# A hybrid decoder layer: its front ordered by a list scheduler, conv sums in PSUM, q over both partition halves

## The chip, the core and the metric

The kernel runs on one core of a Trainium2 chip. The metric is device microseconds of one execution, as the median of several runs. TensorE does the matrix products, VectorE and ScalarE work on SBUF and PSUM, GpSimd works on SBUF alone, and SyncE (SP) issues the loads. Each engine takes its instructions in the order in which the kernel was written, so the place of an instruction in its engine's queue matters as much as its length.

## What is computed

One decoder layer on 512 tokens of width 1024, all in float32. The mixer has an attention group of 8 heads of 64 (with 512 tokens and blocks of 256 it comes to causal softmax attention) and a conv group of 512 channels with 31 taps. Both are joined by one output projection. An MLP with a squared ReLU follows, then a last norm.

```python
xn = rms_norm(h, g_mix_norm)
q, k, v, u = split(xn @ w_in, [512, 1024, 1536])        # u: 1024 columns, a and gate
attn = moba_attention(partial_rope(q), partial_rope(k), v)
a, gte = split(u + b_glu, 2)
c = causal_depthwise_conv(a * sigmoid(gte), w_dw) + b_dw   # 31 taps, 512 channels
conv = swish(layer_norm(c))
h = h + concat([attn, conv]) @ w_out
ff = square(relu(rms_norm(h, g_mlp_norm) @ w_mlp_in))
return rms_norm(h + ff @ w_mlp_out, g_final)
```

## The kernel before

Every large product keeps float32 precision by splitting both operands into a high and a low part and doing three matmuls (`mm3`, lines 158 to 160). A weight unit is 128 x 1024: SP loads it into one of four `raw` buffers, ScalarE copies the high part `wh` (line 115) and VectorE subtracts to get the low part `wl` (line 116, `split_unit`); there are three buffers of parts.

The front, up to the output projection, runs in this order. x is transposed and split into `xh` and `xl`. Units 0 to 7 give the u columns (`u`), from which `glu` makes four gated conv inputs `hin` of 128 channels x 512 tokens each. Units 8 to 11 give q, 12 to 15 k, 16 to 19 v, each in four PSUM banks, one for 128 tokens. q and k are scaled into SBUF by ScalarE (line 396), rotated by VectorE (lines 402 to 405), transposed on TensorE (line 411) and split again (lines 416, 419). A pair of heads shares 128 partitions: the low part `ql` of a head lies on its own 64, and the high part of q is copied to the other half as well by two transfers that GpSimd issues (line 422). Attention then works on 32 groups (head, 128 tokens): scores (lines 467 to 469: q high with the high and low halves of k, q low on 64 partitions with k high, and the mask), row maximum (476), exponential (483), normalisation on GpSimd (491), transpose (497), split of the probabilities (512, 518), and per head the product with v (530, 531). Half of the output projection (k = 0 to 3, the attention rows) is laid between these; the other half follows with the conv rows.

The conv: blocks 0 and 2 belong to GpSimd. For each tap ScalarE makes a product `ct` (line 313) and GpSimd adds it to the sum in SBUF (line 323). Blocks 1 and 3 belong to VectorE, one instruction a tap: `hin` times the tap plus the sum, all in SBUF (line 300; the first tap is line 294). Both are background work, put between other instructions by `background`, which hands each engine a share of the time of every `mm3` by constants from the table `T`. The attention part is an event list: each step has a place in slots (constants of `T`, such as `rm`, `ex`, `pt`), and the sorted list is the order of issue on all engines. All eight PSUM banks are one rotating pool.

After the front the MLP runs in four chunks (`ff`, `z`), TensorE without a gap, weights split two units ahead.

Of the kernel before, what the change touches and what calls it, by code (L numbers as in the profile page):

```python
# [31 lines left out]
POOL_BLOCKS = (0, 2)  # L32
CHUNK = 8
LAG = 3
# [16 lines left out]
T = {"sh_u": 0.608, "sh_p": 0.984, "c_p": 1.34, "sh_q": 0.576, "sh_k": 0.408, "sh_v": 0.308, "rm": 0.077, "ex": 1.057, "no": 1.206, "pt": 3.026, "ph": 3.551, "pl": 3.667, "vm0": 0.073, "vms": 0.365, "sp18": -2.63, "sp19": 4.368, "tk18": 1.875, "tk19": 4.562, "td0": 0.346, "tds": 0.755, "tp0": 0.806, "tps": 1.188, "mt": 10.032, "vs0": 8.08, "vss": 0.464, "sp20": 5.876, "sp21": 17.846, "sp22": 22.437, "sp23": 35.926, "lst": 0.496, "lsc": 2.037, "lbs": 0.564, "ms": 0.818, "msp": 1.662, "lt0": 15.178, "lb0": 24.678, "sw0": 44.304, "y030": 39.415, "y130": 39.247, "lt1": 19.058, "lb1": 23.299, "sw1": 42.879, "y031": 43.841, "y131": 43.064, "lt2": 20.23, "lb2": 23.114, "sw2": 32.77, "y032": 47.586, "y132": 45.976, "lt3": 20.62, "lb3": 26.779, "sw3": 35.787, "y033": 41.198, "y133": 43.882, "va0": 10.623, "va1": 12.961, "va2": 16.592, "va3": 19.269, "va4": 25.479, "va5": 27.641, "va6": 33.134, "va7": 35.475, "y000": 21.654, "y100": 34.028, "y001": 18.594, "y101": 35.235, "y002": 21.974, "y102": 35.427, "y003": 28.582, "y103": 38.359, "y010": 22.511, "y110": 35.552, "y011": 22.65, "y111": 35.891, "y012": 26.772, "y112": 36.197, "y013": 30.362, "y113": 42.111, "y020": 32.483, "y120": 36.489, "y021": 31.142, "y121": 37.522, "y022": 31.744, "y122": 38.63, "y023": 33.118, "y123": 38.744, "el18": 1, "el19": 0, "el20": 1, "el21": 1, "el22": 1, "el23": 0, "epl0": 0, "epl1": 0, "ems": 1, "esh": 0, "esw": 1, "er0": 0, "er1": 0, "er2": 0, "er3": 0, "rx": 31.357, "px": 0}  # L51
# [3 lines left out]
def hybrid_layer(ctx: ExitStack, tc: tile.TileContext, x, pack, w_in, w_out, g_mlp, w1, w2, g_fin, out):  # L55
# [6 lines left out]
    def acc(name):  # L62
        return psum.tile([P, 512], F32, tag="ps", name=name)

    def bank(name):
        return psum.tile([P, 512], F32, tag="ps", name=name)
# [27 lines left out]
    RAW, SPL = 4, 3  # L94

    def load_unit(pieces=1, between=None):
        n = len(raws)
        if n < len(srcs):
            raw = perm.tile([P, 1024], F32, tag="raw", name=f"raw{n}", bufs=RAW)
# [6 lines left out]
            raws[n] = raw  # L106

    def split_unit(pieces=1, low=nc.vector, between=None):
        n = len(parts)
        if n < len(srcs):  # L110
            hi = perm.tile([P, 1024], FR, tag="wh", name=f"wh{n}", bufs=SPL)
            lo = perm.tile([P, 1024], FR, tag="wl", name=f"wl{n}", bufs=SPL)
# [6 lines left out]
            a = srcs[n].shape[1]  # L119
            parts[n] = (hi.rearrange("p (a b) -> p a b", a=a), lo.rearrange("p (a b) -> p a b", a=a))  # L120
            load_unit()

    def resident_unit(hi, lo):
        n = len(parts)
        raw = raws[n].rearrange("p (a b) -> p a b", a=srcs[n].shape[1])
        nc.scalar.copy(hi, raw)
        eng(f"er{n % 4}").tensor_tensor(lo, raw, f32(hi), op=OP.subtract)
        parts[n] = None
        nunit[0] += 1
        load_unit()  # L130
# [10 lines left out]

    bgq = {"dve": deque(), "pool": deque()}
    credit = {"dve": 0.0, "pool": 0.0}
    share = {"dve": T["sh_u"], "pool": T["sh_p"]}

    def background(us):
        for e, q in bgq.items():
            credit[e] += us * share[e]
            while q and credit[e] >= q[0][0]:
                cost, fn = q.popleft()  # L150
                credit[e] -= cost
                fn()
            if not q:
                credit[e] = min(credit[e], 0.0)

    def mm3(ps, sh, sl, mh, ml, first, last):
# [4 lines left out]
        background(3 * mh.shape[-1] / 2400)  # L161
# [5 lines left out]

    xt = x_tiles("x")
    pk = perm.tile([P, C_END], F32, name="pk")
# [57 lines left out]
    pa = phA.enter_context(tc.tile_pool(name="pa", bufs=1))  # L227


    xh = perm.tile([P, KD, S], FR, tag="xh", name="xh")  # L230
# [24 lines left out]
    def norm1(t):  # L255
        junk = pa.tile([P, D], F32, tag="ptah", name=f"junk{t}", bufs=2)
# [6 lines left out]
    def scales_on_rows():  # L263

        rb = acc("rb")
# [21 lines left out]
    hins, accs = {}, {}  # L287
# [5 lines left out]
    def conv_first(e, acc, i, j, bias):  # L293
        e.tensor_scalar(acc, hins[i][:, j:j + S], wtap(i, j), bias, op0=OP.mult, op1=OP.add)

    def conv_dve(i, j):
        if j == 0:
            conv_first(nc.vector, accs[i], i, 0, pk[:, C_BDW + i:C_BDW + i + 1])
# [5 lines left out]
    AHEAD = 2  # L304
    pool_taps, products = [], []

    def product(n):
        if n < len(pool_taps):
            acc, i, j, first = pool_taps[n]
            tmp = None  # L310
            if not first:
                tmp = pa.tile([P, S], F32, tag="ctmp", name=f"ct{i}_{j}", bufs=AHEAD + 2)
                nc.scalar.activation(tmp, hins[i][:, j:j + S], AF.Copy, scale=wtap(i, j))  # L313
            products.append(tmp)

    def conv_pool(n):
        while len(products) < min(n + 1 + AHEAD, len(pool_taps)):
            product(len(products))
        acc, i, j, first = pool_taps[n]
        if first:  # L320
            conv_first(nc.gpsimd, acc, i, j, pk[:, C_BDW + i:C_BDW + i + 1] if j == 0 else 0.0)
        else:
            nc.gpsimd.tensor_tensor(acc, acc, products[n], op=OP.add)  # L323

    def add_taps(e, i, js, acc):
        for n, j in enumerate(js):
            if e == "pool":
                pool_taps.append((acc, i, j, n == 0))
                bgq[e].append((T["c_p"], lambda n=len(pool_taps) - 1: conv_pool(n)))
            else:  # L330
                bgq[e].append((0.67, lambda i=i, j=j: conv_dve(i, j)))

    def glu(i, zg, za):
        sg = pa.tile([P, S], F32, tag="sg", name=f"sg{i}", bufs=1)
        nc.vector.tensor_mul(sg, zg, rbc)
        nc.scalar.activation(sg, sg, AF.Sigmoid, bias=pk[:, C_BG + 4 + i:C_BG + 5 + i])
        hin = hins[i]
        nc.vector.tensor_mul(hin[:, TAPS - 1:], za, rbc)
        nc.vector.scalar_tensor_tensor(hin[:, TAPS - 1:], hin[:, TAPS - 1:], pk[:, C_BG + i:C_BG + i + 1], sg,
                                       op0=OP.add, op1=OP.mult)  # L340
        accs[i] = pa.tile([P, S], F32, tag="acc", name=f"acc{i}", bufs=4)
        if i in POOL_BLOCKS:
            add_taps("pool", i, range(TAPS), accs[i])
            return
        nd = TAPS - (int(T["px"]) if i == 3 else 0)
        add_taps("dve", i, range(nd), None)
        if nd < TAPS:
            more = pa.tile([P, S], F32, tag="ol", name=f"more{i}", bufs=2)
            add_taps("pool", i, range(nd, TAPS), more)
            join.append(lambda: nc.vector.tensor_add(accs[i], accs[i], more))  # L350

    join = []
    for i in range(4):
        hins[i] = pa.tile([P, TAPS - 1 + S], F32, tag="hin", name=f"hin{i}", bufs=4)
# [5 lines left out]
    tx = [acc(f"tx1{b}") for b in range(4)]  # L360
# [5 lines left out]
    block(z[0], w[0], xh, xl, H1)  # L366
    split_unit()
    block(z[1], w[1], xh, xl, H1)
    glu(0, z[0], z[1])
    split_unit()  # L370
    block(z[2], w[2], xh, xl, H1)
    for n in range(3, 8):
        zn = bank(f"u{n}")
        block(zn, unit(), xh, xl)
        z.append(zn)
# [224 lines left out]
    def take(n):  # L600
        U[n] = unit(0)

# [297 lines left out]
```

## Time and profile before

| | |
|---|---|
| median of 3 runs | 624.48 us (624.02 to 624.49) |
| profiled execution | 623.05 us, its span 621.3 us |
| TensorE busy | 578.2 us (93%), 2768 matmuls |
| VectorE busy | 369.7 us (59%) |
| ScalarE busy | 266.1 us (43%) |
| GpSimd busy | 162.9 us (26%) |

The page's chain of work that ended last is 76% TensorE and 15% VectorE, and its largest line is not a matmul: it is line 300, VectorE's conv taps, with 10% of the span. The shares of busy time are means over stages that differ; the rows below cut the span into such stages. A busy TensorE is not one at its peak: successive starts of matmuls show the pace.

### The profile page before, as it was taken

How to read it: one execution, taken by the hardware profiler on the slowest of the kernel's cores; microseconds unless marked ns; L12 is line 12 of the kernel's file. 1: busy time of each engine (PE TensorE's matmuls, PEld its weight loads, DVE VectorE, ACT ScalarE, POOL GpSimd, SP SyncE). 2: the span in 40 equal slices, each digit the busy share in tenths (PEclk: the TensorE clock that was granted, in tenths of full speed). 3: DMA queues.
4: the chain of work that ended last, by engine and by line, in shares of the span. 5: the costliest groups of instructions: out<-in, count | busy, mean ns of one | idle time of the engine just before them, and what ended most of it. 6: DMA issues, size and time to landing. Idle time of an engine off the chain costs nothing.

```text
span 621.3 us, 7312 instructions
## 1 busy us (share of the span) xinstructions
PE 578.2 (93%) x2768; PEld 476.7 (77%) x2768; DVE 369.7 (59%) x486; ACT 266.1 (43%) x445; POOL 162.9 (26%) x170
## 2 busy tenths in 40 slices
PE   8998692876999999999999999999999999999995
PEld 7986562765767788898888888888888888888884
DVE  4589999999989766746424454431455343345243
ACT  6864263663768773435321144322234222334233
POOL 2496598492887551100000000000000000000002
PEclk9999987896999999999999999999999999999998
DMA  8632122161111156205233322233232333222203
GB/s 265 153 98 66 38 68 67 35 135 34 56 47 35 35 205 169 69 1 170 101 102 101 93 78 102 102 102 101 72 99 101 103 101 102 86 86 99 69 0 137
DMA packets 59380, 57.22 MB, mean 92 GB/s; under 512 B 1872, under 2 KB 42960, under 8 KB 59344
## 3 DMA queue, kind: packets, MB, share of 16 engines
q1 hardware_dynamic: 58512, 54.64, 28.6%
q0 software_dynamic: 544, 1.05, 1.0%
q10 hardware_dynamic: 288, 1.05, 0.4%
q8 instruction: 22, 0.36, 0.2%
q14 instruction: 14, 0.11, 0.1%
HBM read 53.59 MB, written 2.10 MB: 90 GB/s over the span
## 4 chain that ended last, share of the span: by engine, by line
PE 76%; DVE 15%; issue 3%; ACT 2%; POOL 2%; DMA 1%; SPq 0%; POOLq 0%; ACTq 0%; DVEq 0%
DVE acc L300 10%; PE ff L159 9%; PE ff L158 9%; PE ff L160 9%; PE z L159 9%; PE z L158 9%; PE z L160 9%; DVE wl L116 3%; PE y L158 2%; PE y L160 2%; PE y L159 2%; PE u L160 1%; PE u L159 1%; PE u L158 1%; PE pt L497 1%
## 5 line engine op out<-in xcount | busy, mean ns | idle before, releaser
L116 DVE TENSOR_TENSOR wl<-raw,wh 128x1024 fp32r<-128x1024 f32 (+1 forms) x86 | 113.2, 1318 | 100.6 <-ACT wh L115 100.3
L115 ACT CAST wh<-raw 128x1024 fp32r<-128x1024 f32 (+1 forms) x94 | 92.6, 991 | 117.8 <-PE z L160 75.3
L323 POOL TENSOR_TENSOR acc<-acc,ct 128x512 f32<-128x512 f32 x60 | 98.2, 1636 | 23.2 <-ACT ct L313 19.5
L158 PE MATMUL ff<-hTh,wh 128*128 128x512 f32 (+1 forms) x280 | 103.9, 371 | 0.0
L159 PE MATMUL ff<-hTl,wh 128*128 128x512 f32 (+1 forms) x280 | 103.8, 371 | 0.0
L160 PE MATMUL ff<-hTh,wl 128*128 128x512 f32 (+1 forms) x280 | 103.8, 371 | 0.0
L159 PE MATMUL z<-wl,ffh 128*128 128x512 f32 (+1 forms) x264 | 101.0, 383 | 0.0
L158 PE MATMUL z<-wh,ffh 128*128 128x512 f32 (+1 forms) x264 | 101.0, 383 | 0.0
L160 PE MATMUL z<-wh,ffl 128*128 128x512 f32 (+1 forms) x264 | 101.0, 383 | 0.0
L699 POOL TENSOR_SCALAR ms0f<-ms_f 128x1 f32<-128x1 f32 x4 | 0.8, 192 | 328.7 <-ACT f L223 328.7
L300 DVE SCALAR_TENSOR_TENSOR acc<-hin,pk,acc 128x512 f32<-128x512 f32 x60 | 83.0, 1384 | 1.4
L763 DVE TENSOR_TENSOR sq<-rl 128x512 f32<-128x512 f32 x32 | 22.2, 692 | 64.3 <-ACT rl L761 64.3
L158 PEld LDWEIGHTS ff<-hTh,wh 128*128 128x128 f32 x280 | 52.8, 188 | 9.1
L160 PEld LDWEIGHTS ff<-hTh,wl 128*128 128x128 f32 x280 | 52.7, 188 | 9.0
L159 PEld LDWEIGHTS ff<-hTl,wh 128*128 128x128 f32 x280 | 52.8, 188 | 9.0
L158 PEld LDWEIGHTS z<-wh,ffh 128*128 128x128 f32 x264 | 49.6, 188 | 9.8
L160 PEld LDWEIGHTS z<-wh,ffl 128*128 128x128 f32 x264 | 49.6, 188 | 9.7
L159 PEld LDWEIGHTS z<-wl,ffh 128*128 128x128 f32 x264 | 49.6, 188 | 9.6
L761 ACT ACTIVATE rl<-ff 128x512 f32<-128x512 f32 x32 | 19.2, 599 | 82.6 <-PE ff L160 82.6
L313 ACT ACTIVATE ct<-hin,pk 128x512 f32<-128x512 f32 x60 | 41.5, 719 | 17.9 <-POOL acc L323 17.5
L765 DVE TENSOR_TENSOR ffl<-sq,ffh 128x512 fp32r<-128x512 f32 x32 | 22.2, 693 | 21.9 <-ACT ffh L764 21.9
L764 ACT CAST ffh<-sq 128x512 fp32r<-128x512 f32 x32 | 19.8, 620 | 25.5 <-DVE sq L763 25.5
(162 smaller groups left out, 899.5 us busy)
## 6 DMA issues: line engine op xcount, KB each, us to landing
raw<-w SPq DMA_DIRECT2D x64, 512.0 KB, 3.9
raw<-w_in SPq DMA_DIRECT2D x18, 512.0 KB, 3.7
raw<-w_out SPq DMA_DIRECT2D x8, 512.0 KB, 3.7
xr<-x SPq DMA_DIRECT2D x4, 512.0 KB, 5.0
out<-ot SPq DMA_DIRECT2D x8, 256.0 KB, 2.0
x<-x SPq DMA_DIRECT2D x4, 256.0 KB, 4.4
raw<-w_in SPq DMA_DIRECT2D x4, 256.0 KB, 5.9
x<-x SPq DMA_DIRECT2D x2, 512.0 KB, 6.9
```

The source lines that it names most:

```text
L115: nc.scalar.copy(hi[:, c], raws[n][:, c])
L116: low.tensor_tensor(lo[:, c], raws[n][:, c], f32(hi[:, c]), op=OP.subtract)
L158: nc.tensor.matmul(ps, sh, mh, start=first, stop=False)
L159: nc.tensor.matmul(ps, sh, ml, start=False, stop=False)
L160: nc.tensor.matmul(ps, sl, mh, start=False, stop=last)
L300: nc.vector.scalar_tensor_tensor(accs[i], hins[i][:, j:j + S], wtap(i, j), accs[i], op0=OP.mult, op1=OP.add)
L313: nc.scalar.activation(tmp, hins[i][:, j:j + S], AF.Copy, scale=wtap(i, j))
L323: nc.gpsimd.tensor_tensor(acc, acc, products[n], op=OP.add)
L761: nc.scalar.activation(rl, ps, AF.Relu)
L763: nc.vector.tensor_mul(sq, rl, rl)
L764: nc.scalar.copy(ff["h"][:, b], sq)
L765: nc.vector.tensor_sub(ff["l"][:, b], sq, f32(ff["h"][:, b]))
```

## The change

Four things are done to the front; the MLP stays as it is.

- The order. A class `Plan` holds every step of the front from the second half of u to the output projection's first half, with the engine (or two engines to choose from), an estimated duration, the steps it needs and the buffers it uses. `run` is a list scheduler that works at build time: of the steps that can start earliest it takes the one with the longest remaining path. The kernel then issues the steps in that order. `background`, the event list and the table `T` go. Splits of weights may go to VectorE or GpSimd.
- The conv sums of VectorE's blocks 1 and 3 lie in a PSUM bank while they grow; the last tap writes to SBUF. GpSimd's blocks 0 and 2 stay in SBUF.
- q is copied twice side by side for each head before its transpose, so that the high and the low part (`ql`, now 8 heads x 512 tokens on 128 partitions) fill both halves of the partitions. Each 128 tokens of q take 8 transposes instead of 4, and GpSimd's two transfers go. A score takes two full 128-row matmuls and the mask.
- PSUM banks and the buffers of weights get names of their own, so that the scheduler can give them out. Some tiles move in SBUF (the tiles called `shift`), and the scratch for transfers issued by GpSimd is set to 4096.

```diff
+class Plan:
+    def step(self, engines, cost, fn, needs=(), uses=(), bias=0.0, keep=0, shared=False, hot=False):
...
+    def run(self):
+        for s in reversed(self.steps):
+            s["tail"] = min(s["eng"].values()) + max([n["tail"] for n in s["next"]], default=0.0) + 0.1
...
+            e0 = min(best, key=lambda x: x[2])[1]
+            a0 = min(x[2] for x in best if x[1] == e0)
+            s, e, a, c = max((x for x in best if x[1] == e0 and x[2] <= a0 + 0.02), key=lambda x: x[0]["tail"] + x[0]["bias"])
...
-    psum = ctx.enter_context(tc.tile_pool(name="psum", bufs=8, space=bass.MemoryType.PSUM))
+    psum = ctx.enter_context(tc.tile_pool(name="psum", bufs=1, space=bass.MemoryType.PSUM))
...
-        background(3 * mh.shape[-1] / 2400)
...
+        l = plan.step({"dve": 1.23, "pool": 2.2}, 0, lambda: low(nc.gpsimd if l["eng_used"] == "pool" else nc.vector),
+                      needs=[h], uses=[rb, wb], shared=True)
...
-            nc.vector.scalar_tensor_tensor(accs[i], hins[i][:, j:j + S], wtap(i, j), accs[i],
-                                           op0=OP.mult, op1=OP.add)
...
+        cs = ps_buffer(f"cs{i}")
...
+            s = plan.step("dve", 0.8, lambda src=src, j=j, last=last: nc.vector.scalar_tensor_tensor(
+                get(acc) if last else get(cs), src, wtap(i, j), get(cs), op0=OP.mult, op1=OP.add),
+                needs=[s], uses=[cs, acc] if last else [cs])
...
-    ql = pa.tile([P, 4, S], FR, name="ql")
+    ql = pa.tile([P, NH, S], FR, name="ql")
...
+            src = get(b).rearrange("p (h d) -> p h d", h=NH).unsqueeze(2).to_broadcast([P, NH, dup, HD])
+            nc.scalar.activation(tile_of(), src, AF.Copy, scale=rq[t] if nm == "q" else rs[t])
...
-                nc.gpsimd.dma_start(qs[own[1 - a], a::2], qs[own[a], a::2])
...
-        nc.tensor.matmul(sp[:, 0:n], ql[rows, h // 2, tok], ks[rows, h, 0:n], start=False, stop=False)
+                nc.tensor.matmul(p[:, 0:n], ql[:, h, tok], ks[:, h, 0:n], start=False, stop=False)
...
+            s = pe_step(2 * mm(n) + BF16_MASK, scores, uses=[sp], chain=False, keep=KEEP,
+                        needs=[qready[qt, a]] + [kready[t, h % 2] for t in range(qt + 1)] + score_steps[-1:])
...
+                fin.append(pe_step(3 * mm(512), omm, needs=[l, mixready[k]], uses=[y[hf][t], wb], chain=False, keep=KEEP_Y))
...
+    plan.step("sp", 7.0, reload_x, needs=score_steps)
+    order = plan.run()
+    for s in order:
+        s["fn"]()
```

`keep` (2 for scores, 3 for the output projection) is the number of PSUM banks that must stay free before such a step may take one while a head's product with v is outstanding.

## Rows read from the trace of the kernel before

**Rows 1.** The page's busy table: us, share of the span, instructions, by engine.

```profile
PE 578.2 (93%) x2768; PEld 476.7 (77%) x2768; DVE 369.7 (59%) x486; ACT 266.1 (43%) x445; POOL 162.9 (26%) x170
```

**Rows 2.** Stretches: us, busy us (instructions) by engine, TensorE's granted clock, DMA share.

```profile
21.00:57.00 36.00, 35.75 (x192) 30.71 (x190) 29.53 (x25) 18.23 (x27) 24.89 (x15) 1.00 0.28 79
57.00:178.00 121.00, 89.77 (x360) 68.75 (x361) 117.35 (x140) 67.35 (x111) 85.95 (x55) 0.86 0.23 64
178.00:239.00 61.00, 59.99 (x332) 46.44 (x331) 47.52 (x106) 45.71 (x105) 35.54 (x47) 1.00 0.25 87
239.00:613.00 374.00, 374.00 (x1757) 313.84 (x1756) 163.55 (x190) 117.89 (x168) 6.96 (x22) 1.00 0.30 92
```

**Rows 3.** Waits, 57 to 178 us: who waited for whom, us, times, longest.

```profile
PE tpq L411 <- DVE qf L405: 10.0, 1, 10.0
...
PE tpk L411 <- DVE kf L405: 9.2, 1, 9.2
```

**Rows 4.** Groups by line, 57 to 178 us: busy us, mean ns, idle before.

```profile
L300 DVE SCALAR_TENSOR_TENSOR acc<-hin,pk,acc 128x512 f32<-128x512 f32 x52 | 70.5, 1356 | 1.1
L116 DVE TENSOR_TENSOR wl<-raw,wh 128x1024 fp32r<-128x1024 f32 x11 | 20.6, 1876 | 0.4 <-ACT wh L115 0.4
...
L469 PE MATMUL s<-maskb,identb 128*128 128x128 bf16 x9 | 2.1, 230 | 0.0
```

**Rows 5.** Single lines, 21 to 239 us: ns min/median/max, first and last start.

```profile
L300 DVE SCALAR_TENSOR_TENSOR acc<-hin,pk,acc x60: 734/1651/2089, 40.9 to 176.3; 128x512 f32<-128x512 f32 x60
...
L116 DVE TENSOR_TENSOR wl<-raw,wh x17: 1199/2160/2316, 24.8 to 226.3; 128x1024 fp32r<-128x1024 f32 x17
...
L338 DVE TENSOR_TENSOR hin<-u,rbc x4: 681/687/692, 26.7 to 74.5; 128x512 f32<-128x512 f32 x4
...
L610 DVE SCALAR_TENSOR_TENSOR vhl<-v,r,vhl x4: 725/730/739, 177.1 to 179.9; 128x512 fp32r<-128x512 f32 x4
```

**Rows 6.** Timeline of GpSimd and VectorE near 100 us: start, us, what.

```profile
94.07 12.73 POOL L323 TENSOR_TENSOR acc<-acc,ct 128x512 f32<-128x512 f32 x7
...
96.65 6.83 DVE L300 SCALAR_TENSOR_TENSOR acc<-hin,pk,acc 128x512 f32<-128x512 f32 x4
...
107.12 3.12 DVE L300 SCALAR_TENSOR_TENSOR acc<-hin,pk,acc 128x512 f32<-128x512 f32 x4
```

**Rows 7.** Timeline of TensorE and its weight loads around one score group.

```profile
187.01 0.60 PE L497 MATMUL pt<-ident,pr 128*128 128x128 f32 x4
...
187.37 0.47 PE L467 MATMUL s<-ks,qs 128*128 128x512 f32 x1
...
187.77 0.18 PEld L468 LDWEIGHTS s<-ks,ql 64*128 64x128 f32 x1 [0.24 <-issue]
187.77 0.50 PE L468 MATMUL s<-ks,ql 64*128 64x512 f32 x1
...
188.20 0.23 PE L469 MATMUL s<-maskb,identb 128*128 128x128 bf16 x1
```

**Rows 8.** Timeline of TensorE in q's projection, after a wait.

```profile
79.07 0.63 PE L159 MATMUL q<-wl,xh 128*128 128x512 f32 x1
79.50 0.63 PE L160 MATMUL q<-wh,xl 128*128 128x512 f32 x1
```

**Rows 9.** Timeline of TensorE in a product with v.

```profile
181.43 0.39 PE L531 MATMUL o<-pl,vhl 128*128 128x512 f32 x1
181.66 0.34 PE L530 MATMUL o<-ph,vhl 128*128 128x384 f32 x1
```

**Rows 10.** Groups by line and shape, whole span: busy us, mean ns, idle before.

```profile
L571 DVE TENSOR_SCALAR y<-cp,mv,r_ln 128x512 f32<-128x512 f32 x4 | 3.1, 798 | 0.0
...
L396 ACT ACTIVATE qf<-q,rq 128x512 f32<-128x512 f32 x4 | 2.4, 681 | 0.0
...
L422 POOL DMA_DIRECT2D qs<-qs x2 | 1.5, 737 | 1.6 <-ACT qs L416 1.6
```

**Rows 11.** Score matmuls of the high part: ns min/median/max, first and last start.

```profile
L467 PE MATMUL s<-ks,qs x32: 220/350/473, 153.2 to 217.7; 128*128 128x128 f32 x8, 128*128 128x256 f32 x8, 128*128 128x384 f32 x8, 128*128 128x512 f32 x8
```

More of the change, by code (lines that the diff above doesn't have):

```diff
@@ L304, in hybrid_layer @@
[L304 to L323, printed above, removed]
@@ L359, in hybrid_layer @@
     block(z[1], w[1], xh, xl, H0)
-    tx = [acc(f"tx1{b}") for b in range(4)]
+    tx = [bank(f"tx1{b}") for b in range(4)]
     transpose_half(1, tx)
@@ new lines, in hybrid_layer, with u_block, part @@
+    zs, zdone = {}, {}
+    def u_block(n, cols):
+        if n not in zs:
+            zs[n] = held("ps", f"b{n}", z[n]) if n < 3 else ps_buffer(f"u{n}")
+        wb, l = U[n]
+        width = cols.stop - cols.start
+        def part(k0):
+            hi, lo = parts[n]
+            for k in (k0, k0 + 1):
+                mm3(get(zs[n])[:, cols], hi[:, k], lo[:, k], xh[:, k, cols], xl[:, k, cols], k == 0, k == KD - 1)
+        for k0 in range(0, KD, 2):
+            zdone[n] = pe_step(6 * mm(width), lambda k0=k0: part(k0), needs=[l], uses=[zs[n], wb])
@@ L408, in rope_transpose, with project, one @@
-    def rope_transpose(nm, t, qf):
-        tp = bank(f"tp{nm}{t}")
-        for p in range(4):
-            nc.tensor.transpose(tp[:, p * P:(p + 1) * P], qf[:, p * P:(p + 1) * P], ident)
-        tv = tp.rearrange("p (a b) -> p a b", a=4)
+    new_pr = pa_buffers("pr", PR, [P, S])
+    rt = pa.tile([P, 2, NH, 2, HALF], F32, name="rope")
+    rope_last = [None]
+    def project(nm, u0):
+        bk = [ps_buffer(f"{nm}{t}") for t in range(NT)]
+        done = {}
+        def one(t, k):
+            hi, lo = parts[u0 + k // 2]
+            ts = slice(t * P, (t + 1) * P)
+            mm3(get(bk[t]), xh[:, k, ts], xl[:, k, ts], hi[:, k % 2], lo[:, k % 2], k == 0, k == KD - 1)
+        order = [(t, k) for k in range(4) for t in range(NT)] + [(t, k) for t in range(NT) for k in range(4, KD)]
+        for t, k in order:
+            wb, l = U[u0 + k // 2]
+            done[t] = pe_step(3 * mm(512), lambda t=t, k=k: one(t, k), needs=[l], uses=[bk[t], wb])
+        return bk, done
@@ L456, in eng @@
-    def eng(k):
-        return nc.gpsimd if T[k] > 0.5 else nc.vector
-    slots = [(h, qt) for h in range(NH) for qt in range(NT)]
-    scored, probs, pT, tps = {}, {}, {}, {}
-    def scores(h, qt):
-        rows = own[h % 2]
-        n = (qt + 1) * P
-        tok = slice(qt * P, (qt + 1) * P)
-        sp = bank(f"s{h}{qt}")
-        nc.tensor.matmul(sp[:, 0:n], qs[:, h, tok], ks[:, h, 0:n], start=True, stop=False)
-        nc.tensor.matmul(sp[:, 0:n], ql[rows, h // 2, tok], ks[rows, h, 0:n], start=False, stop=False)
-        nc.tensor.matmul(sp[:, tok], identb, maskb, start=False, stop=True)
-        nm = stat(f"nm{h}{qt}")
-        scored[h, qt] = sp, nm
@@ L493, in prob_transpose, with flip @@
-    def prob_transpose(h, qt):
-        pr, _ = probs.pop((h, qt))
-        tp = bank(f"pt{h}{qt}")
-        for j in range(qt + 1):
-            nc.tensor.transpose(tp[:, j * P:(j + 1) * P], pr[:, j * P:(j + 1) * P], ident)
-        tps[h, qt] = tp
+            tp = ps_buffer(f"tpq{t}{a}")
+            def flip(a=a, tp=tp):
+                for h in range(4):
+                    c = (4 * a + h) * P
+                    nc.tensor.transpose(get(tp)[:, h * P:(h + 1) * P], get(qb)[t % 2][:, c:c + P], ident)
@@ L520, in hybrid_layer @@
-    mix, outs = {}, {}
-    def values(h):
-        ph, pl = pT.pop(h)
-        op = bank(f"o{h}")
-        outs[h] = op
-        for j in range(NT):
-            seen = slice(PSTEP * j + j * P, PSTEP * j + S)
-            v = vhl[:, j, h].rearrange("p a d -> p (a d)")
-            nc.tensor.matmul(op[:, j * P:], v, ph[:, seen], start=j == 0, stop=False)
-            nc.tensor.matmul(op[:, j * P:], v, pl[:, seen], start=False, stop=j == NT - 1)
-    def mix_sum(h):
+    lasts_exp, mixready, score_steps = [], {}, []
@@ L675, in reload_x @@
+    plan.step("pe", 22.0, lambda: None, needs=fin + list(mixready.values()))
     def reload_x():
@@ L721, in transpose_tile @@
     def transpose_tile(t, src):
-        tps = [acc(f"th{t}{b}") for b in range(2)]
+        tps = [bank(f"th{t}{b}") for b in range(2)]
         for c in range(KD):
@@ L830, in hybrid_layer @@
             pieces += [(NT - 1, slice(0, 256)), (NT - 1, slice(256, 512))] if final else [(NT - 1, slice(0, 512))]
-            banks = [acc(f"z{c}{hf}{n}") for n in range(len(pieces))]
+            banks = [bank(f"z{c}{hf}{n}") for n in range(len(pieces))]
             tail = CHUNK - 4 if final else CHUNK
```

710 lines of the change are left out of this document (439 added, 271 removed).

## Prediction

> **What bounds the kernel now.** I read the busy table first: TensorE is the busiest engine by far, VectorE 59% [rows 1]. That average hides where time is lost, so I cut the span into stretches at the places where the work changes [rows 2]. From 239 to 613 us (second half of the output projection, MLP) TensorE is busy without a gap at full clock: 374 us in which VectorE has 210 us to spare. Nothing in the change touches that work, so I carry it over unchanged. From 21 to 57 us (the u columns) TensorE is dense as well, 35.75 of 36. From 178 to 239 (the rest of attention, first half of the output projection) it is dense again, 59.99 of 61. The loss sits in one place: from 57 to 178 (q, k, v, first scores) TensorE is busy 89.8 of 121 us at a mean granted clock of 0.86, while VectorE is busy 117.35.
>
> The waits of that stretch say why [rows 3]: TensorE stood 10.0 us for VectorE's rotation of q and 9.2 us for that of k. VectorE runs its queue in order, and in front of the rotations and of the weights' low parts (wl) lie conv taps. After each such gap TensorE restarts at the lower of its two levels: the same matmuls start 0.43 us apart [rows 8] where at full clock they start 0.23 apart [rows 9]. So the queue of VectorE sets the middle stretch.
>
> What fills that queue is 52 taps of line 300 at a mean of 1.356 us and 11 splits of line 116 at 1.876 [rows 4]. Yet a tap can take 0.734 and a split 1.199 [rows 5]. Rows 6 show what decides: while GpSimd adds products back to back (94.1 to 106.8 us, seven in 12.73), four taps take 6.83; right after it stops, four take 3.12, or 0.78 each. GpSimd's adds read two SBUF tensors, and so do taps and splits. VectorE operations that read PSUM and one SBUF tensor do not stretch: line 338 runs 681 to 692 ns (26.7 to 74.5 us, where GpSimd is busy some 70% of the time [rows 2]) and line 610, the same kind of instruction as a tap, 725 to 739 [rows 5].
>
> **The change part by part.** *Taps in PSUM.* A tap then reads one SBUF tensor and PSUM, the operands that did not stretch. No row shows VectorE writing PSUM, so I bound the price: 0.73 (the fastest tap) from below, 0.80 (line 571, which reads PSUM) from near [rows 10], and 1.356 if nothing changes. I take 0.78, the tap with GpSimd silent [rows 6]. In the middle stretch: 52 x (1.356 - 0.78) = 30 us off VectorE. The splits still read two SBUF tensors; they may fall to 1.199 or stay at 1.876; I take 1.55, as GpSimd's adds will fill less of the time: 11 x 0.33 = 3.6 off (0 to 7.4). VectorE's load there goes from 117.35 to 83.8.
>
> [...]
>
> In the stretch before (21 to 57) the other 8 taps get 0.58 shorter too, 4.6 us, and VectorE idles 6.5 us there. The scheduler can pull taps from the middle into that room as soon as the gated inputs exist; I take 5 us (0 to 11), so the middle holds 79 us of VectorE work.
>
> *The order.* The list scheduler gives each engine its free step with the longest remaining path. Splits and rotations have the projections and all of attention behind them, so they come ahead of taps, and the 10 us waits of [rows 3] should go. What is late next is TensorE itself. Its floor for the middle: 288 projection matmuls at 0.227 = 65.4; 48 transposes (16 of them new) at 0.09, from the four in 0.36 of [rows 7], = 4.3; nine score groups [rows 4] at some 0.72 = 6.5; with the first probability transposes about 78 us. So TensorE (78) and VectorE (79) are then equally loaded, and ScalarE holds 67 us of work in the same stretch [rows 2]. Three engines that feed each other with static queues don't overlap perfectly. Bounds for the waits: 0, and the 31 us that TensorE stood there before. I take 10, since the dense stretches show 1 us of waiting in 61 with one engine loaded and here three are. The middle becomes 88.5 instead of 121: 32.5 us gained, 43 at most.
>
> *q in both halves.* Score matmuls now stream a 64-row weight (line 468) between 128-row ones. Its load shows 0.24 us in which the weight queue waits for nothing the profile shows, and the matmuls start 0.40 and 0.43 apart at 512 columns [rows 7], where 128-row pairs of the same width start 0.23 apart [rows 9]. With ql over all 128 partitions both gaps could fall by 0.17 and 0.20, or neither. 23 of the 32 groups lie in the dense stretch after 178 us: 23 x 0.37 = 8.5 at most, 0 at least. The first gap has its like in [rows 9], the second ends at a bf16 matmul and has none; I take 4.
>
> [...]
>
> The price of this part: 16 transposes (counted), and the copy of q becomes 1024 columns wide on ScalarE, at most another 0.68 us for each of four [rows 10], 2.7 in all, hidden in ScalarE's 54 idle us of the middle (its price if that cover is gone). It removes the two transfers issued by GpSimd (line 422, 0.74 us each of its queue [rows 10]) which stood in GpSimd's queue between adds; they had no waiter I can see, so I take nothing.
>
> *The rest at nothing.* Loads on SP keep their order and four buffers, hidden behind 77% idle DMA in the middle [rows 2]. The reload of x stays behind the last scores; from there to the end of the front there are 21 us now [rows 2, 11] and some 15 afterwards, which hides it; uncovered, it would stop the first residual add for what is missing. Named PSUM banks, moved tiles and the smaller scratch change no instruction of the MLP; cost 0 while banks are free (the last rival has the other end).
>
> **Sum.** Profiled run 623.05 us (span 621.3 and 1.75 around it). 623.05 - 32.5 - 4 = 586.5. The median of the runs is 624.48, 1.4 above the profiled one; on that footing 588.
>
> **The rivals.** [...]
>
> *Waits eat more.* If the scheduler's durations are off, each of the three full engines waits in order for another, 20 to 31 us instead of 10: 598 to 609, and up to 618 if the restarts at the lower clock stay too (of the 43 us that TensorE loses there today, 12 are slow clock). For it: three engines above 75% load. Against: most durations in the rows are steady to a few per cent.
>
> *More than I take.* Waits near 0 and scores cheaper by 8: 571 to 580. For it: the first stretch has 11 us of room on VectorE.
>
> *It doesn't do what it says.* The pairing with GpSimd goes by the kind of instruction or by the write, taps stay at 1.356, VectorE's load remains 117 in the middle and only the order helps: TensorE's waits move but VectorE still ends last, 623 to 626. Against: line 610 [rows 5].
>
> *Slower: banks.* Conv sums hold a PSUM bank for most of the front and output sums take others, so that score and transpose tiles queue for the last ones. Now the 32 score groups start from 153.2 to 217.7 us [rows 11], 2.08 apart. If they start at some 122, the last comes as late as now at 3.1 apart; at 3.6 apart it comes 16 us later, 640. It decides from 3.1 on. For it: eight banks, one or two gone to taps. Against: the scheduler keeps two or three free while attention runs.
>
> **How the numbers follow.** Forecast (580 to 597): 0.45. Loads exposed, 592: 0.15. More: 0.10. Waits: 0.18. Doesn't do it: 0.04. Banks: 0.08. The likeliest gives 588. The range from 573 to 610 leaves out some 3% below and 17% above. A measurement here tells 0.2% (1.2 us) from no change: faster 0.88, same 0.04, slower 0.08.
>
> **What would show it.** Taps at 0.75 to 0.80 while GpSimd adds; adds near 1.3; TensorE's wait for the rotations under 2 us and a clock of 0.95 or more through q, k and v; score matmuls at 512 columns 0.23 apart; the MLP still 374 us. I am wrong if taps stay above 1.2, if TensorE waits over 25 us between 57 us and the first output matmuls, or if the MLP's dense stretch grows.

## The result and the profile after

The changed kernel takes **614.41 us** (median of 4 runs, 612.14 to 615.64); the kernel before, on the same chip, 624.25 us. The ratio is 0.9839, 95% interval 0.9804 to 0.9873: about 10 us faster, where 588.0 was forecast with a range of 573 to 610. The direction was right, the time lies outside the range, and the gain is a quarter of what was forecast. The profiled execution took 615.64 us, its span is 613.9.

The stretches of [rows 2], now of the kernel after: length, busy us (instructions) of TensorE, its weight loads, VectorE, ScalarE and GpSimd, TensorE's granted clock, DMA share, GB/s.

```profile
21.00:57.00 36.00, 36.00 (x198) 31.38 (x197) 26.95 (x28) 22.54 (x32) 26.45 (x18) 1.00 0.30 88
57.00:178.00 121.00, 98.31 (x427) 78.08 (x425) 101.02 (x159) 71.66 (x119) 88.67 (x70) 0.86 0.20 62
178.00:239.00 61.00, 57.24 (x315) 46.14 (x316) 39.15 (x85) 40.34 (x96) 22.20 (x32) 1.00 0.30 95
239.00:613.00 374.00, 367.53 (x1728) 308.49 (x1726) 163.31 (x193) 117.96 (x167) 7.93 (x23) 1.00 0.29 90
```

VectorE has 16 us less to do from 57 to 178 us, TensorE does 8.5 us more there, and its clock is no better. Fixed edges hide what happened, for the work has moved across them. So I took milestones instead: the last matmul of v's projection, the last one of the first part of the output projection (y, the four attention blocks of both column halves), and the first MLP matmul (ff). Each is a single line of TensorE's timeline (ns min/median/max, first to last start). Of the kernel before:

```profile
L158 PE MATMUL v<-wh,xh x32: 387/397/775, 133.7 to 177.5; 128*128 128x512 f32 x32
L158 PE MATMUL y<-wh,mixh x32: 389/389/481, 193.5 to 237.9; 128*128 128x512 f32 x32
L158 PE MATMUL ff<-hTh,wh x280: 277/389/396, 263.1 to 568.9; 128*128 128x512 f32 x116, 128*128 128x256 f32 x24
```

And of the kernel after:

```profile
L250 PE MATMUL v<-wh,xh x32: 389/393/776, 121.7 to 152.2; 128*128 128x512 f32 x32
L250 PE MATMUL y<-wh,mixh x32: 389/389/479, 206.9 to 230.8; 128*128 128x512 f32 x32
L250 PE MATMUL ff<-hTh,wh x280: 280/389/396, 256.0 to 561.8; 128*128 128x512 f32 x116, 128*128 128x256 f32 x24
```

The last matmul of v comes 25.3 us earlier (177.5 to 152.2). From there to the last y matmul the kernel before takes 60.4 us and the one after 78.6: 18.2 us are given back. What remains is 7.1 us at the first MLP matmul, and behind it both take the same (358.2 and 357.9 us to the end of the span). The output projection shows where to look: before, its first matmul comes 16.0 us after the last of v, with 13 of attention's 32 score groups still to come; after, 54.7 us later, behind the last scores (204.7).

Groups of the kernel after that answer to [rows 4]: busy us, mean ns, idle before.

```profile
L554 DVE SCALAR_TENSOR_TENSOR cs<-hin,pk,cs 128x512 f32<-128x512 f32 x58 | 43.6, 752 | 1.3
L445 DVE TENSOR_TENSOR wl<-raw,wh 128x1024 fp32r<-128x1024 f32 x15 | 27.5, 1839 | 11.0 <-ACT wh L441 11.0
L538 POOL TENSOR_TENSOR acc<-acc,ct 128x512 f32<-128x512 f32 x60 | 90.5, 1508 | 7.1 <-ACT ct L535 2.6
```

The taps do what was hoped (0.752 us against 1.356). The splits stay at 1.839, GpSimd's adds take 1.508. Waits of the kernel after (who waited for whom: us, times, longest), ScalarE's over the whole span, TensorE's from 57 to 178 us as in [rows 3]:

```profile
ACT ct L535 <- POOL acc L538: 28.7, 32, 1.5
...
PE tpk L682 <- DVE kf L646: 5.6, 1, 5.6
PE pt L773 <- POOL pr L768: 4.9, 1, 4.9
```

The wait for q's rotation is gone, that for k's is 5.6, and a new wait follows v: probability transposes for GpSimd's normalisation. The chain of waits around it (start us, us, what):

```profile
151.62 0.29 DVE nm L762
151.92 0.67 DVE cs L554
...
156.57 0.76 DVE cs L554
157.50 0.70 POOL pr L768
158.24 1.12 PE pt L773 x4
159.36 0.87 PE cp L829 x4
160.25 0.71 DVE bn L835
161.53 0.56 POOL r_ln L310
```

When v's matmuls end, conv taps are still in VectorE's queue (8 start from 151.8 on), the reciprocals stand behind them, GpSimd's normalisation behind those, and then the conv's LayerNorm comes before the next scores. The 20 us around this place, same columns as the first view:

```profile
150.00:170.00 20.00, 12.36 (x53) 9.63 (x53) 16.75 (x37) 7.15 (x17) 10.53 (x16) 0.65 0.16 53
```

TensorE is busy 12.36 of 20 at a mean granted clock of 0.65 and ScalarE 7.15. The 20 us after v's end in the kernel before are dense, 19.03 busy at 1.00:

```profile
178.00:198.00 20.00, 19.03 (x115) 14.23 (x114) 17.18 (x47) 15.96 (x44) 14.19 (x22) 1.00 0.04 13
```

### The profile page after: what moved, and what is told of

The parts are those of the page before. It is cut to its first block, busy times and chain, and to the rows that moved or that the text cites. A ratio compares the mean times of both kernels' runs of the same rounds, so it can differ in the third digit from the quotient of the medians.

```text
span 613.9 us, 7318 instructions
## 1 busy us (share of the span) xinstructions
PE 577.5 (94%) x2784; PEld 480.9 (78%) x2784; DVE 339.7 (55%) x484; ACT 267.6 (44%) x445; POOL 153.4 (25%) x170
## 3 DMA queue, kind: packets, MB, share of 16 engines
q1 hardware_dynamic: 58512, 54.64, 28.7%
## 4 chain that ended last, share of the span: by engine, by line
PE 75%; POOL 13%; issue 3%; DVE 3%; ACT 3%; DMA 1%; SPq 0%; POOLq 0%; ACTq 0%; DVEq 0%
POOL acc L538 12%; PE ff L250 10%; PE ff L251 10%; PE ff L252 9%; PE z L250 9%; PE z L251 9%; PE z L252 9%; PE y L250 2%; PE y L252 2%; PE y L251 2%; PE s L755 1%; PE v L250 1%; PE pt L773 1%; PE v L251 1%; PE v L252 1%
## 5 line engine op out<-in xcount | busy, mean ns | idle before, releaser
L224 DVE TENSOR_TENSOR wl<-raw,wh 128x1024 fp32r<-128x1024 f32 (+1 forms) x69 | 81.4, 1183 | 93.9 <-ACT wh L223 93.8
L223 ACT CAST wh<-raw 128x1024 fp32r<-128x1024 f32 (+1 forms) x73 | 71.0, 981 | 112.1 <-PE z L252 79.9
L538 POOL TENSOR_TENSOR acc<-acc,ct 128x512 f32<-128x512 f32 x60 | 90.5, 1508 | 7.1 <-ACT ct L535 2.6
L535 ACT ACTIVATE ct<-hin,pk 128x512 f32<-128x512 f32 x60 | 42.4, 720 | 29.5 <-POOL acc L538 28.7
L554 DVE SCALAR_TENSOR_TENSOR cs<-hin,pk,cs 128x512 f32<-128x512 f32 x58 | 43.6, 752 | 1.3
L989 DVE TENSOR_TENSOR ffl<-sq,ffh 128x512 fp32r<-128x512 f32 x32 | 22.2, 692 | 22.0 <-ACT ffh L988 22.0
L445 DVE TENSOR_TENSOR wl<-raw,wh 128x1024 fp32r<-128x1024 f32 x15 | 27.5, 1839 | 11.0 <-ACT wh L441 11.0
```

The source lines that it names most:

```text
L223: nc.scalar.copy(hi[:, c], raws[n][:, c])
L224: low.tensor_tensor(lo[:, c], raws[n][:, c], f32(hi[:, c]), op=OP.subtract)
L445: e.tensor_tensor(lo, raws[n], f32(hi), op=OP.subtract)
L535: p = plan.step("act", 0.72, lambda src=src, j=j, ct=ct: nc.scalar.activation(get(ct), src, AF.Copy, scale=wtap(i, j)), needs=[ready, prod ...
L538: s = plan.step("pool", 1.29, lambda ct=ct: nc.gpsimd.tensor_tensor(get(acc), get(acc), get(ct), op=OP.add), needs=[p, s], uses=[acc, ct])
L554: s = plan.step("dve", 0.8, lambda src=src, j=j, last=last: nc.vector.scalar_tensor_tensor(get(acc) if last else get(cs), src, wtap(i, j), ...
```

## The experiments

Two theories at first. **Pace:** GpSimd's adds run slower than the scheduler was told (1.508 us against 1.29), ScalarE's products wait for their four buffers (28.7 us above), and weight casts and so VectorE's splits queue behind them. **Attention:** the list order puts the long-path projections first and leaves attention without cover. Before either could be tested, the parts of the change had to be priced. Runs e1 to e4 stand beside a kernel before of 624.21 us, e5 to e8 of 622.47, e9 to e11 of 622.57, e12 of 623.7, e13 and e14 of 623.5; brackets hold 95% intervals of the ratio to it. These values of the same kernel differ by up to 1.8 us, so a difference in us between two runs can be off by as much; where it matters, the ratios are compared as well. "Old order" is the order of the kernel before.

**e1: GpSimd's adds cut short** (changed kernel).

```diff
-nc.gpsimd.tensor_tensor(get(acc), get(acc), get(ct), op=OP.add)
+nc.gpsimd.tensor_tensor(get(acc)[:, 0:P], get(acc)[:, 0:P], get(ct)[:, 0:P], op=OP.add)
```

> The changed kernel in the same order, but GpSimd adds only 128 of the 512 columns of each conv product (the sums of blocks 0 and 2 are left incomplete); ScalarE still makes the whole product. Theory ring: GpSimd's adds take 1.51 us where the order was made for 1.29, and ScalarE, which has four product buffers, is held to that pace, with the high parts of the weights behind the products. Then ScalarE's 28.7 us of waits for GpSimd go to under 3, v ends near 133 us instead of 152.6, and the time falls by 15 to 22 us, to 592 to 599. Rival splits: the loss is VectorE's own splits, 1.84 us beside an add instead of 1.23; then 15 splits save 9 us at most, 605 or more. Rival attention: the projections end earlier but attention still stands behind VectorE's taps, and less than 8 us reach the end, 606 or more.

593.34 us, 0.9515 [0.9481, 0.9549]: 21 us less. The edit takes away both the adds' length and what they cost others: splits fall to 1.223 us.

```profile
L445 DVE TENSOR_TENSOR wl<-raw,wh 128x1024 fp32r<-128x1024 f32 x15 | 18.3, 1223 | 10.5 <-ACT wh L441 10.5
```

But the milestones say that nearly the whole gain, 20.6 of the 22.5 us up to the last y matmul, lies ahead of v's end (152.2 to 131.6). The stretch behind it still takes 76.7 us.

**e2: VectorE's sums back in SBUF** (changed kernel).

```diff
-get(acc) if last else get(cs), src, wtap(i, j), get(cs), op0=OP.mult, op1=OP.add),
+get(acc), src, wtap(i, j), get(acc), op0=OP.mult, op1=OP.add),
```

> The changed kernel in the same order, but the conv sums of VectorE's blocks 1 and 3 lie in SBUF again. It prices the PSUM part inside the new order. Taps go from 0.75 to 1.3 to 1.6 us while GpSimd adds, adds from 1.51 to 1.65 or more. Theory ring (GpSimd sets the pace, taps in PSUM give it back only part): 625 to 640, slower than the kernel before. If VectorE has room to spare in the new order: 615 to 622.

645.57 us, 1.0344 [1.0313, 1.0376], beyond both expectations: the PSUM part is worth 31 us in the new order, and without it the change is slower than the kernel before. The same taps on SBUF operands:

```profile
L554 DVE SCALAR_TENSOR_TENSOR acc<-hin,pk,acc 128x512 f32<-128x512 f32 x60 | 83.4, 1389 | 1.3
```

**e3: q's low part on 64 partitions** (changed kernel).

```diff
-nc.tensor.matmul(p[:, 0:n], ql[:, h, tok], ks[:, h, 0:n], start=False, stop=False)
+nc.tensor.matmul(p[:, 0:n], ql[own[h % 2], h, tok], ks[own[h % 2], h, 0:n], start=False, stop=False)
```

> The changed kernel in the same order, but the low part of q is used from 64 partitions only, as before (same numbers, 64-row weights for that one matmul of each score). Score matmuls go back from 0.31 and 0.24 us apart to 0.40 and 0.43 at 512 columns, 0.3 us a group. If TensorE bounds attention, as the prediction had it: 32 x 0.3 = up to 9 us slower, 620 to 624. If attention waits for the other engines: 0 to 3 us slower, 614 to 617.

631.33 us, 1.0103 [1.006, 1.0146], again beyond both expectations: q's part is worth 17 us in the new order. Of it 13.8 us lie behind v's end (78.6 to 92.4 us), where TensorE stays at the lower of its two levels, a granted clock of 0.50, for 30 us:

```profile
160.00:190.00 30.00, 25.56 (x84) 16.83 (x84) 19.45 (x51) 9.27 (x31) 9.42 (x21) 0.50 0.07 23
```

**e4 and e5: the change without its order.** e4 is the kernel before with VectorE's sums in a PSUM bank of their own; e5 adds q's low part on both halves (copied by SP's queue). e5 computes all of the reference.

```diff
-nc.vector.scalar_tensor_tensor(accs[i], hins[i][:, j:j + S], wtap(i, j), accs[i],
+nc.vector.scalar_tensor_tensor(accs[i] if j == TAPS - 1 else cs[i], hins[i][:, j:j + S], wtap(i, j), cs[i],
...
-nc.gpsimd.dma_start(qs[own[1 - a], a::2], qs[own[a], a::2])
+nc.sync.dma_start(f32(qs[own[1 - a], a::2]), f32(qs[own[a], a::2]))
+nc.sync.dma_start(f32(ql[own[1 - a], a::2]), f32(ql[own[a], a::2]))
```

> The kernel before with its own order; only VectorE's conv sums lie in a PSUM bank (one of the eight kept for them, seven for the rest; the last of the output banks takes the kept one). The PSUM part alone. VectorE's taps go from 1.38 to 0.76 us: 36 us of its queue. As the prediction's step on the middle stretch had it: TensorE's waits for splits and rotations shrink by most of that, 595 to 605. Theory ring: here too ScalarE waits for GpSimd (17.5 us before), so GpSimd's pace remains: 606 to 616. If seven banks are too few, 620 or more.

> The old order with everything of the change but the order: conv sums in PSUM and both parts of q on both halves of the partitions (the halves are exchanged by four transfers that SP issues, in place of GpSimd's two). Old order and PSUM alone took 598.1 us. If the full-height low part of q is worth in the old order what the groups' matmul starts say (0.3 us a group, TensorE dense): 589 to 596. If it is worth nothing where TensorE keeps its full clock: 597 to 600. Either way 14 to 25 us below the changed kernel, which would then be the price of the new order; if the price is elsewhere, 606 or more.

e4: 598.12 us, 0.9578 [0.9544, 0.9613]. e5: **591.23 us, 0.9495 [0.9475, 0.9515]**. So in the old order PSUM sums bring 26 us and q's part 7 (5 by the ratios), and the list order, the third part, **costs** 23 us (21 by the ratios). This price takes in two things that e5 does not share with the changed kernel: there q gets to the other half by 16 more transposes and wider copies instead of SP's transfers, and all banks have names; neither was run apart. e5 beats both kernels. Its milestones:

```profile
L161 PE MATMUL v<-wh,xh x32: 389/397/774, 111.7 to 146.8; 128*128 128x512 f32 x32
L161 PE MATMUL y<-wh,mixh x32: 387/391/502, 160.9 to 206.6; 128*128 128x512 f32 x32
```

Of the 24 us between 230.8 and 206.6, 5.4 lie ahead of v's end and 18.8 behind it. The stretch behind v's end, after and e5 (same columns as the first view):

```profile
152.20:230.80 78.60, 65.58 (x354) 52.12 (x353) 59.23 (x133) 48.08 (x118) 34.73 (x50) 0.89 0.25 81
```

```profile
146.80:206.60 59.80, 56.07 (x330) 45.00 (x329) 47.96 (x108) 45.31 (x106) 33.91 (x45) 1.00 0.25 82
```

In the changed kernel TensorE is idle 13.0 us of this stretch and 0.89 of the clock is granted; in e5 it is idle 3.7 us at 1.00.

**e6, e7, e8: single cures in the list order.** e6 tells the scheduler 1.6 us for an add, e7 gives the products seven buffers in the same order, e8 puts the reciprocals first.

```diff
-s = plan.step("pool", 1.29, lambda ct=ct: nc.gpsimd.tensor_tensor(
+s = plan.step("pool", 1.6, lambda ct=ct: nc.gpsimd.tensor_tensor(
...
+            return pa.tile([P, S], F32, tag=f"ctr{ring[0] % 7}", name=name)
...
-get(rc), get(sm)), needs=[s], uses=[sm, rc])
+get(rc), get(sm)), needs=[s], uses=[sm, rc], bias=60.0)
```

> The changed kernel; the scheduler is told 1.6 us for one of GpSimd's adds instead of 1.29 (the trace has 1.51 and a gap of 0.07), nothing else. Theory ring: with the true pace the products stand later in ScalarE's queue and the weights' high parts ahead of them; ScalarE's waits for GpSimd fall from 28.7 to under 12 us, v ends 8 to 13 us earlier (near 141), the time is 600 to 608. If the pace of the adds itself is the limit, whatever the order: 611 to 616.

> The changed kernel in the same order with seven product buffers instead of four. ScalarE can then run three more products ahead of GpSimd. Theory ring: by the end of the adds GpSimd is some 16 us behind the order; three buffers are 3 x 1.58 = 4.7 us of that: 608 to 611. If ScalarE's waits are idle time that costs nothing: 613 to 615.5.

> The changed kernel; the reciprocal of each group's sum gets a bias of 60 in the scheduler, so that VectorE does it ahead of conv taps. Theory attention: in the changed kernel the first groups stand from 127 to 157 us because their reciprocals lie behind taps in VectorE's queue (GpSimd's normalisation waits 24.5 us for them), TensorE falls to its lower clock near 160, and attention takes 82 us instead of 65. With the reciprocals first: products with v start 8 us or more before 169, and the time is 602 to 610. If attention is held by something else (conv's end, PSUM banks): 612 to 617.

e6: 611.75 us, 0.982 [0.98, 0.9839], the figure of its rival. e7: 610.23, 0.9797 [0.9774, 0.982], as the ring theory had it. e8: 612.48, 0.9855 [0.9817, 0.9893], the figure of its second expectation. Each is within some 4 us of the changed kernel, and the intervals overlap with its own (0.9804 to 0.9873). e6 and e7 bring v's end forward (146.8 and 148.4) and leave the stretch behind it (78.6 and 77.8). In e8 the reciprocals now lie among the last taps, but there TensorE waits for the last tap itself (its LayerNorm transposes, 4.0 us), and 150 to 170 us looks the same (12.11 busy, clock 0.66).

**e9: e5 with the short adds.** The edit of e1 on e5, which closes a square of two orders and two paces.

```diff
-nc.gpsimd.tensor_tensor(acc, acc, products[n], op=OP.add)
+nc.gpsimd.tensor_tensor(acc[:, 0:P], acc[:, 0:P], products[n][:, 0:P], op=OP.add)
```

> The old order with all sums of VectorE in PSUM and q in both halves (591.23 us), and GpSimd's adds cover only 128 of 512 columns, so three quarters of what GpSimd adds to the convolution are left out. With e1, the changed kernel and e5 this makes a square of two orders and two paces of GpSimd. If the list order alone can't bear GpSimd's pace, and the old one has room for it: 584 to 590 us. If GpSimd's adds cost both orders alike, some 21 us as between the changed kernel and e1: 568 to 574, and then the list order costs its 20 us in another way, in attention.

578.15 us, 0.9279 [0.9261, 0.9297], between the two expectations. GpSimd's pace costs the list order 21.1 us (614.41 to 593.34) and the old order 13.1 (591.23 to 578.15); the list order costs 23.2 us with full adds and 15.2 with short ones. So 8 of the 23 us go with the pace (7 of 21 by the ratios), and 15 have another cause. They lie behind v's end: with short adds v ends 1.9 us earlier in the list order than in the old one (131.6 and 133.5), and the stretch behind it is 17.0 us longer (76.7 and 59.7).

**e10 and e11: truth and room.** e10 is e7 with the scheduler told 1.5 us an add and 1.84 a split; e11 is e5 with six product buffers in place of four.

```diff
-l = plan.step({"dve": 1.23, "pool": 2.2}, 0,
+l = plan.step({"dve": 1.84, "pool": 2.2}, 0,
...
-tmp = pa.tile([P, S], F32, tag="ctmp", name=f"ct{i}_{j}", bufs=AHEAD + 2)
+tmp = pa.tile([P, S], F32, tag="ctmp", name=f"ct{i}_{j}", bufs=AHEAD + 4)
```

> The changed kernel, with its scheduler told 1.5 us for each of GpSimd's adds (1.508 in the trace) and 1.84 for each split of VectorE (1.839), and seven product buffers in place of four. If the list order runs late because of these two durations and the tight buffers, and the plan holds once it is told the truth: the dense stretch begins some 15 us earlier than in the changed kernel, 597 to 602 us. If something else makes it late (the order within attention): 607 to 612, as with either step alone.

> The old order with sums in PSUM and q in both halves (591.23 us), and six product buffers in place of four between ScalarE and GpSimd. ScalarE waits there for GpSimd 17.2 us. If those waits hold up the weights behind them: 586 to 589 us. If the old order has cover for them: 590 to 592, no change that can be told.

e10: 610.27 us, 0.9791 [0.9764, 0.9817], the rival's figure. v ends at 146.6 as in e5, so durations and room cure what the list order loses ahead of v's end (a longer add alone, e6, does it too); the stretch behind it takes 79.3. The edit does not quite tell the truth about the splits: `run` adds up to 0.9 us to a split that starts ahead of the end of GpSimd's planned work, so a split told as 1.84 can be planned at 2.74, where the trace has 1.839 on average. e11: 590.61, 0.9475 [0.9454, 0.9496], no change that can be told from e5.

**e12: e5 with a late output projection.** The first three of y's four blocks in its first columns moved to the last product with v (9 of the 36 matmuls run just ahead of it, from 187.9 us, the others behind it).

```diff
-at(T[f"y0{k}{t}"], omm, y0, t, k, 20 + k // 2, k % 2)
+at(max(T[f"y0{k}{t}"], 35.6 if k < 2 else 36.0), omm, y0, t, k, 20 + k // 2, k % 2)
```

> The old order with sums in PSUM and q in both halves (591.23 us), with one thing taken from the list order: the first three quarters of the output sums' first columns (36 matmuls, 8.2 us at 0.227) no longer lie among the attention but behind its last product with v, as in the changed kernel. If attention is bound by its chain through VectorE, ScalarE and GpSimd, and the output projection is what fills TensorE there: these 8 us come on top, 597 to 600 us. If TensorE's time there is needed by attention itself, or the banks that the sums held are worth as much: 590 to 593 us.

595.56 us, 0.9571 [0.9531, 0.9611]: some 4.5 us slower than e5, between the two. The stretch grows by 4.9 us (59.8 to 64.7). In the list order y waits, among other things, for a step of ScalarE with a short path behind it, the copy of attention's sums to y's operand. In the changed kernel, and then in e5:

```profile
L811 ACT CAST mixh<-os x4: 617/644/670, 199.6 to 216.4; 128x512 fp32r<-128x512 f32 x4
```

```profile
L551 ACT CAST mixh<-os x4: 619/620/628, 155.9 to 197.2; 128x512 fp32r<-128x512 f32 x4
```

The first product with v comes at 168.9 us and at 148.9, so the first copy follows 30.7 us later in the one and 7.0 in the other. Not all of that is the copy's place in the queue. A copy needs the sums of two heads, and VectorE's second addition to them (line 806) ends at 189.6 us in the changed kernel: at least 20.7 of the 30.7 us pass in attention itself, and at most 10.0 are the copy's own wait. The scheduler's `keep`, which holds y back while too few PSUM banks are free, is a rival that no run tested.

**e13 and e14: the gap behind v** (changed kernel). e13 leaves out VectorE's last eight taps of the last block; e14 keeps all work, with reciprocals first and the LayerNorm behind attention. In both the scheduler orders the steps anew.

```diff
-conv_out[i] = taps_dve(i, range(TAPS), ready, acc, bias_dw(i))
+conv_out[i] = taps_dve(i, range(TAPS - 8 if i == 3 else TAPS), ready, acc, bias_dw(i))
...
-uses=[cp] + list(accs.values()), chain=False)
+uses=[cp] + list(accs.values()), chain=False, bias=-30.0)
```

> The changed kernel with 8 of the 62 conv taps of VectorE left out (the last eight of the last channel block), so that output isn't the reference's there. In the changed kernel 8 taps and the conv's normalisation behind them run after the last matmul of v, and the stretch from there to the last output matmul of the first half takes 78.6 us against 60 in the old order, whatever GpSimd's adds cost. If these leftover taps in VectorE's queue make that stretch long: 69 to 73 us for it and 602 to 606 in all. If the stretch is long for its own order (output projection behind all of attention, static order of the steps): 76 to 79 us for it, 609 to 613 in all.

> The changed kernel with the scheduler told to put reciprocals first and the conv's normalisation (its transposes and roots) behind the attention's steps, all work kept. If the chain of leftover taps, reciprocals and normalisation standing in front of the attention makes TensorE's gap after v (12.4 us busy of 20 from 150 to 170 us, at 0.65 of the clock): the gap shrinks by some 5 us of idle time and 3 of slow clock, 605 to 608. If attention in list order leaves TensorE idle anyway, since the output projection is no longer there to fill it: 610 to 613.

e13: 608.05 us, 0.9755 [0.9728, 0.9783], and 72.9 us for the stretch: 5.7 less, within the first expectation for the stretch, though the whole time lies between the two. e14: 612.63 us, 0.982 [0.9794, 0.9846], 78.3 for the stretch, 12.68 us busy of 150 to 170 at 0.67: with the LayerNorm elsewhere the gap stays; TensorE then waits 4.0 us for the last tap at its probability transposes.

The milestones side by side (us; worked out from the same rows of each trace):

| kernel | last v | last y | between | median |
|---|---|---|---|---|
| before | 177.5 | 237.9 | 60.4 | 624.25 |
| after | 152.2 | 230.8 | 78.6 | 614.41 |
| e1, list order, short adds | 131.6 | 208.3 | 76.7 | 593.34 |
| e10, list order, told, 7 buffers | 146.6 | 225.9 | 79.3 | 610.27 |
| e13, list order, 8 taps less | 149.8 | 222.7 | 72.9 | 608.05 |
| e4, old order, PSUM sums alone | 150.8 | 213.0 | 62.2 | 598.12 |
| e5, old order | 146.8 | 206.6 | 59.8 | 591.23 |
| e9, old order, short adds | 133.5 | 193.2 | 59.7 | 578.15 |
| e12, old order, late y | 145.8 | 210.5 | 64.7 | 595.56 |

The "between" column goes by the order and hardly by GpSimd's pace: 60 to 62 in the old order as it was, 77 to 79 in the list order with all its work.

## Why the prediction was right in direction and wrong in size

**Taps: right.** Forecast 0.78, measured 0.752 (741 to 756 ns), and no tap stretched while GpSimd added. The tap in PSUM is 18 ns above the quickest tap of [rows 5] (752 and 734).

**Splits and adds: mis-sized.** Splits were taken at 1.55 and are 1.839, near the upper bound: 15 of them, 4.3 us of VectorE. "Adds near 1.3" was wrong: 1.508, 12.5 us over 60. They still stretch each other: half of the splits take 2.06 us or more, as they took 2.16 or more before, for 90.5 us of adds now lie in a shorter stretch, beside the splits.

**The order: the step that failed.** Two claims stood there. First, the middle was to fall by 32.5 us, part of it because the order would remove the waits of [rows 3]. It fell by 25.3, 7.2 less; yet e4, which has the old order and the cheaper taps alone, brings v's end forward by 26.7, and e5 by 30.7. The cheaper taps alone took most of those waits (19.2 us before; in e4 1.5 for q's rotation and 5.8 for k's), and against e5 the new order gave back 5.4, which e10 recovers. Second, and larger: I carried the stretch behind it over from [rows 2] as "dense again", less 4 us for q, while the change was free to reorder it. It was to take 56.4 us by the milestones (60.4 less 4) and took 78.6, 22.2 more. The two together, 29.4, are the miss: the profiled run was to take 586.5 us and took 615.64, 29.1 more.

The stretch was dense because of what the old order laid there. It has the output projection among attention and starts its last tap ahead of the last v matmul (in e5 at 145.1 and 146.8 us). The list order takes the longest remaining path first; as I read its code, what has the shortest paths, the last taps and the copies to y's operand, it leaves to a place where nothing covers them.

Of the 18.2 us by which the stretch grew, leftover taps account for 5.7 (e13, changed kernel) and the late output projection for 4.9 (e12, measured in the old order). A third share is work that no experiment moved: when v ends, the list order has done less of attention. Scores and probability transposes behind v's end, in the changed kernel (152.2 to 230.8) and then in e5 (146.8 to 206.6); count, then busy us, mean ns, idle before:

```profile
L757 PE MATMUL s<-maskb,identb 128*128 128x128 bf16 x27 | 6.5, 240 | 0.0
L773 PE MATMUL pt<-ident,pr 128*128 128x128 f32 x80 | 14.3, 304 | 8.0 <-POOL pr L768 6.0 <-ACT pr L764 1.4 <-DVE pl L782 0.7
```

```profile
L475 PE MATMUL s<-maskb,identb 128*128 128x128 bf16 x23 | 5.3, 230 | 0.0
L503 PE MATMUL pt<-ident,pr 128*128 128x128 f32 x67 | 12.0, 280 | 2.6 <-POOL pr L497 2.3
```

Each group has one mask matmul, so 4 groups and 13 transposes more are left, in e10 and with short adds (e1) as well. At the prediction's own prices, 0.72 and 0.09, that is some 4 us of TensorE, an estimate. These shares come from different orders and need not add up; some 4 us stay open, and so does the part that `keep` and the banks have. That TensorE is idle and at the lower clock right behind v is shown, the share of each step is not. A list order with an early output projection was not run.

**q in both halves: near in size in the old order, in part by luck, and under-priced in the new one.** Forecast 4 (0 to 8.5); e4 to e5 shows 7, or 5 by the ratios. But the forecast put its 4 us into the 23 groups of the dense stretch, and that stretch gave 2.4 (62.2 to 59.8); 4.0 lie ahead of v's end (150.8 to 146.8), where e5 also moved q's transfers from GpSimd to SP, and what they come from is open. In the list order the part is worth 17 (e3), where TensorE was at the lower level for 30 us. In the score group of [rows 7], now with 128 rows:

```profile
178.42 0.48 PE L755 MATMUL s<-ks,qs 128*128 128x512 f32 x1
178.73 0.40 PE L756 MATMUL s<-ks,ql 128*128 128x512 f32 x1
178.97 0.23 PE L757 MATMUL s<-maskb,identb 128*128 128x128 bf16 x1
```

The starts lie 0.31 and 0.24 apart, where they lay 0.40 and 0.43: falls of 0.09 and 0.19, where 0.17 and 0.20 were the most. So this group gained 0.28 us; "Loads exposed" (592 us, 0.15) stood for scores at their old price, which it does not show.

**The rest.** The MLP is unchanged, as forecast (358.2 and 357.9 us). The clock was to be 0.95 or more through q, k and v and is 0.91 from 57 to 152.2 us; the wait for a rotation was to be under 2 us and is 5.6. One of the prediction's signs of being wrong came: TensorE stood idle for 25.9 us between 57 us and the first output matmul at 206.9 (124.01 busy of 149.90), over the 25 named.

```profile
57.00:206.90 149.90, 124.01 (x598) 98.44 (x597) 124.47 (x224) 95.75 (x190) 101.86 (x92) 0.89 0.16 51
```

The rival "waits eat more" (598 to 609, up to 618) came nearest, but its ground, wrong durations, carries only the part ahead of v's end. The banks rival did not come to its price: scores start from 122.8 to 204.7 us, 2.6 apart, under the 3.1 where it would decide; whether banks hold part of the open time was not tested. The other edits taken at nothing were not tested one by one; e5 comes within 3.2 us of the forecast's 588 with only PSUM sums and q's part, so without the order to which the prediction gave part of its gain.

## What to carry to other kernels

A dense stretch is dense because of what the order laid there: when a change is free to reorder it, price its chain anew and ask which independent work will still cover it. A list scheduler that ranks by remaining path can spend the long-path work first and leave the fillers for last, as it did here, and it should be given the durations that hold beside the other engines' work. When a change has several parts, run it with all but one of them: here the third part cost what the range had not held.

## What the runs showed of the hardware

In the kernel after, an add of GpSimd took 1.29 us beside taps whose sums lie in PSUM and 2.16 beside a VectorE split, and that split took 2.31. From the chain of the kernel after, and VectorE's timeline at the same place:

```profile
40.33 2.16 POOL acc L538
42.57 1.29 POOL acc L538
```

```profile
39.03 2.31 DVE L445 TENSOR_TENSOR wl<-raw,wh 128x1024 fp32r<-128x1024 f32 x1
...
42.10 3.13 DVE L554 SCALAR_TENSOR_TENSOR cs<-hin,pk,cs 128x512 f32<-128x512 f32 x4
```

Splits take 1.22 on average where adds are short (e1). So at this place the add was 0.87 us longer and the split 1.09. I had priced the stretch on VectorE's side alone. The second surprise is how long the lower clock can last: in e3 TensorE was busy 25.56 of the 30 us from 160 on at a granted clock of 0.50, its lower level, through all of them. In the changed kernel, which differs in the row count of one matmul a score, the clock was 0.50 from 160 to 170 and 1.00 again from 175 on. What keeps it low in the one and not in the other was not tested.
